# Attention outputs in 64x64 tiles: one block of queries on its own 64 rows, masks on the diagonal squares only

## The chip, the cores and the metric

One Trainium2 chip, one of its NeuronCores. The metric is the device time of one execution of the whole program, in microseconds (us). A run gives the median of several executions; beside it one execution is recorded by the hardware profiler.

Engines are named as in the profile: PE is TensorE (matmuls), PEld its weight loads, DVE is VectorE, ACT is ScalarE, POOL is GpSimd, SP issues most of the transfers.

## The reference

Two layers over 1024 tokens of width 1024: a retention/RWKV layer, then an attention layer, each followed by a SwiGLU network. The change lies in the attention layer alone:

```python
def swa_sink_mixer(h, w_qkv, b_qkv, sinks, w_o, b_o):
    ...
    z = h @ w_qkv + b_qkv
    q, k, v = jnp.split(z, [SWA_WIDTH, SWA_WIDTH + SWA_KV_HEADS * HEAD_DIM], axis=-1)
    ...
    kb, vb = with_prev(k), with_prev(v)
    s = jnp.einsum('bnqhgd,bnkhd->bnhgqk', q, kb).astype(jnp.float32) * HEAD_DIM ** -0.5
    qi = jnp.arange(W)[:, None]
    kj = jnp.arange(2 * W)[None, :]
    rel = qi + W - kj
    band = (rel >= 0) & (rel < W)
    ...
    m = jnp.maximum(jnp.max(s, axis=-1, keepdims=True), sink)
    e = jnp.exp(s - m)
    p = e / (jnp.sum(e, axis=-1, keepdims=True) + jnp.exp(sink - m))
    o = jnp.einsum('bnhgqk,bnkhd->bnqhgd', p.astype(vb.dtype), vb)
    return o.reshape(B, T, SWA_WIDTH) @ w_o + b_o
```

Sixteen heads of 64 in four groups share four key and value heads. Queries come in blocks of 128 (W); a query sees itself and the 127 tokens before it, so of the 256 keys of its own and the previous block exactly 128 are in its window. Cut into squares of 64 queries by 64 keys, a block has eight: two are empty, two are full, and four lie on a diagonal (two of the own block, two of the previous one).

## The kernel before, in words

The attention stage works on two halves of 512 tokens (`hf` 0 and 1). `proj` makes queries, keys and values: 24 matmuls of 512 columns for each of 12 tiles, their weights split into a high and a low part (ACT casts, L431; DVE subtracts, L432), the sum taken out of PSUM by DVE (L1635) and ACT (L1636). `kv` turns the values into token rows `vt` by PE transposes against `c_ident` (L1670), four for each of two value tiles, copied out by ACT (L1671).

The attention itself runs over 16 pairs: half, group of four heads, two blocks of queries. Each pair goes through four steps, which `ATTN_PLAN` writes into the program as S, D, M and O with the pair's number:

- S (`scores`): 24 score matmuls in 64x64 tiles (L1718; 20 where a half begins), into the PSUM banks r, c and two m. ACT copies the keys' part out (L1731), DVE puts the own block's keys over it by a mask (`copy_predicated`, L1732). So one row of 128 slots holds, slot by slot, either the own key or the previous block's. DVE takes the maximum (L1750) and the sink (L1751, L1752); ACT makes eight exponentials with their sums (L1755) and that of the sink (L1753); DVE adds and inverts (L1756, L1757); POOL and DVE multiply half each (L1759); DVE transposes in 32x32 pieces (L1765), and a transfer carries the tile to DRAM.
- D (`fetch`): four transfers bring it back as `pc`, key slots on the partitions.
- M (`sides`): DVE multiplies all 1024 columns by a mask (L1779: own keys); DVE and POOL subtract 512 each (L1784: previous keys). Both sides lie in `pT`.
- O (`out`): eight matmuls (six where a half's first block has no previous one), 128 key slots by 64 head columns by 256 query columns in full fp32, into the bank y (L1797); ACT casts them out (L1803), DVE takes the rest (L1804).

Small letters in `ATTN_PLAN` fill the time between: q, k, r are half-steps of the projections, w the output projection of half 0 (L446 to L449), f the norm that opens the second network (`form0`: `normed` L1247, then `split` L461 and L463), p half-steps of `ffn_early` (its first half is copied out by ACT at L1465 before the second half accumulates).

PE's order in the stage is written out: `K.queue(mark, ATTN_ORDER)` numbers the PSUM tiles in the order of their first use and chains the matmuls as the string says (`17:12` is twelve of tile 17, `18,19:12` twelve in turn from two tiles). The order on the other engines is the scheduler's. Bank f has three buffers, m two, r, c and y one each.

Of the kernel before, what the change touches and what calls it, by code (L numbers as in the profile page):

```python
# [16 lines left out]
P = 128  # L17
# [15 lines left out]
for _n, _w in (  # L33
# [9 lines left out]
    ("dmask", 1024), ("qdec", 512), ("kdec", 8), ("gam", 4), ("amask", 256), ("eps", 4),  # L43
# [9 lines left out]
def make_consts():  # L53
# [45 lines left out]
    put("amask", np.concatenate([np.where(x[:, None] == x[None, :], own, 0.0), own.T], axis=1))  # L99
# [155 lines left out]
class Kern:  # L255
    def __init__(self, ctx, tc, A, out):
# [20 lines left out]
        self.bd = self.dram("bd", [KT, P, HT])  # L277
        self.u0d = self.dram("u0", [NP, 2, P, HT])
# [972 lines left out]
    def form0(self, g, r, n8, sp):  # L1251

        self.X = {nm: [self.hl(n8, k + o) for k in range(4)] for nm, o in (("11", 0), ("21", 4))}
        for k in range(4):
            for nm, kk in (("11", k), ("21", k + 4)):
                f = self.t(sp, [P, HT], "u0", 4)
                self.normed(f, 0, kk, g, r)
                self.nc.sync.dma_start(self.bd[kk], f)
                self.split(f, *self.X[nm][k], False)

# [112 lines left out]
    def ffn_early(self, L, p, sp, banks):  # L1373

        u = self.uses(L, p, sp)
        g = []
        for i, nm in enumerate(("gate", "up")):
            w = self.wload(self.A[f"w_{nm}{L}"][2 * p])
            u0 = self.t(sp, [P, HT], "u0", 4)
# [42 lines left out]
    def ffn_pair(self, L, p, sp, next_w, form, x):  # L1422

        u = self.uses(L, p, sp, x)
        self.nc.sync.dma_start(x["11"], self.hid[2 * L][2 * p])
        u0s, gens = [], []
        for i in range(2):
            u0s.append(self.t(sp, [P, HT], "u0", 4))
# [182 lines left out]
    def attn_open(self, ap):  # L1611
        nc = self.nc
        m = self.const(ap, "amask").rearrange("p (m o t) -> p m o t", m=2, o=1)
        self.own = m[:, 0].rearrange("p o (x t) -> p o x t", x=2).to_broadcast([P, 2, 2, 64]).bitcast(mybir.dt.uint32)
        self.key = m[:, 1].rearrange("p o (q t) -> p q o t", q=4).to_broadcast([P, 4, 8, 32])
# [8 lines left out]
        self.pk = self.pvt = None  # L1624
        self.akv, self.aq, self.ch = {}, ([], []), {}
# [12 lines left out]
    def kv(self, hf, nr, ap):  # L1638
# [4 lines left out]
        vt = self.t(ap, [P, 5, 256], "vt", 2)  # L1643
# [15 lines left out]
        if hf:  # L1659
            G.tensor_copy(vt[:, 0, :], pvt[:, 4, :])  # L1660
        vcs = []
        for i in range(2):
            vc = self.t(self.pp, [P, HT], "nq", 4)
            yield from self.proj(nr, 10 + i, vc, bias=self.col("bqkv", 10 + i))
            vcs.append(vc)
            yield
        for i, vc in enumerate(vcs):
# [16 lines left out]
    def attn(self, ap, outs, fill, plan):  # L1684
# [52 lines left out]
        def scores(j):  # L1737
# [15 lines left out]
            S.activation(es, es, AF.Exp)  # L1753
            for h in range(8):
                S.activation(s8[:, h], s8[:, h], AF.Exp, bias=m[:, h : h + 1], accum_out=den[:, h : h + 1])  # L1755
# [13 lines left out]
        def fetch(j):  # L1769
            pc = pcs[j] = self.t(ap, [P, 4, 8, 32], "pc", 1)  # L1770
            for k in range(4):
                nc.sync.dma_start(
                    pc[32 * k : 32 * k + 32].rearrange("p q h t -> p q (h t)"), ds[j][:, :, k].rearrange("q t x -> t q x")
                )

        def sides(j):
            pc = pcs[j]
            pT = pTs[j] = self.t(ap, [P, 2, 4, 8, 32], "pT", 1)
            x = V.tensor_tensor(out=pT[:, 1], in0=pc, in1=self.key, op=ALU.mult)  # L1779
            if j + 2 in sinks:  # L1780
                self.behind(x, sinks[j + 2])
            for i, e in enumerate((V, G)):
                h = slice(4 * i, 4 * i + 4)
                e.tensor_tensor(out=pT[:, 0, :, h], in0=pc[:, :, h], in1=pT[:, 1, :, h], op=ALU.subtract)  # L1784

        def out(j):
# [16 lines left out]
            S.copy(hi, po)  # L1803
            V.tensor_tensor(out=lo, in0=po, in1=hi.bitcast(F32), op=ALU.subtract)  # L1804
# [65 lines left out]
def trunk(tc, A, out):  # L1870
    with ExitStack() as ctx:
# [106 lines left out]
        def form():  # L1978
            K.form0("n2b", K.factor_of(0, sp, "f"), K.n8(K.pp), sp)
# [23 lines left out]
        close(ga)  # L2003
        gc, cb = K.pool("cb", "right")
# [9 lines left out]
        close(gs, gc)  # L2014
# [68 lines left out]
```

## Time and profile before

| | us |
|---|---|
| median of 3 runs | 2271.2 |
| lowest and highest | 2270.53, 2272.11 |
| the profiled execution, its own time | 2270.19 |
| its span in the trace | 2268.4 |

The busy shares of the page are PE 98%, DVE 74%, ACT 45% and POOL 45% of the span; the TensorE clock is granted at 0.996 on the mean. The attention stage lies between about 1332 and 1640 us of the span. An "idle" number in brackets behind an instruction is the time that its engine stood still just before it, with what ended the wait. Matmuls overlap, so the step from one start to the next tells what one costs, not its own duration.

### The profile page before, as it was taken

The page shows a single profiled execution, that of the slowest core. Times are in us where ns is not written, and L with a number is a line of the kernel's source. Part 1 is how long each engine was busy: PE and PEld are TensorE (multiplying, and loading weights), DVE is VectorE, ACT ScalarE, POOL GpSimd, SP SyncE. Part 2 cuts the span into 40 slices and gives each one's busy share as a digit, 9 for nine tenths or more (in the row PEclk, how much of TensorE's full clock was granted, in tenths as well). Part 3 has the DMA queues.
Part 4 walks back from the last instruction along what each step waited for, and adds up shares of the span by engine and source line. Part 5 has one row for each costly group of instructions (what it writes and reads, how often), then busy time and mean ns, then how long its engine had stood idle before and what let it go on. Part 6 is the DMA issues. An engine that isn't in the chain of part 4 may idle for free. (4 is left out here: it accounts for less than half of the span.)

```text
span 2268.4 us, 36181 instructions
## 1 busy us (share of the span) xinstructions
PE 2222.8 (98%) x13296; PEld 1785.8 (79%) x13296; DVE 1687.9 (74%) x2476; ACT 1012.2 (45%) x1914; POOL 1024.7 (45%) x800
## 2 busy tenths in 40 slices
PE   8999999999999999999999999899899999999998
PEld 6777777778878888888888887687688888888886
DVE  7877965876567358888886868977557788888866
ACT  5454544424455333333333466657344333333336
POOL 3123221202341057777777601214203677777676
PEclk9999999999999999999999999999999999999999
DMA  8565654444456555555667334435446455658663
GB/s 281 186 220 203 201 158 134 141 118 124 147 181 205 185 172 209 209 211 216 237 241 247 130 123 137 154 131 168 163 140 230 177 215 209 211 196 290 228 218 116
DMA packets 181856, 423.22 MB, mean 187 GB/s; under 512 B 44464, under 2 KB 55344, under 8 KB 181680
## 3 DMA queue, kind: packets, MB, share of 16 engines
q1 hardware_dynamic: 178272, 414.37, 53.1%
q10 hardware_dynamic: 2832, 4.45, 0.6%
q8 instruction: 105, 1.72, 0.3%
q0 software_dynamic: 576, 2.10, 0.2%
q14 instruction: 71, 0.58, 0.1%
HBM read 283.87 MB, written 131.60 MB: 183 GB/s over the span
## 5 line engine op out<-in xcount | busy, mean ns | idle before, releaser
L290 PE MATMUL ps_f<-n,w 128*128 128x512 f32 x1440 | 358.8, 403 | 8.8 <-ACT w L431 5.7
L290 PEld LDWEIGHTS ps_f<-n,w 128*128 128x128 f32 x1440 | 266.9, 189 | 83.5 <-issue 12.6
L432 POOL TENSOR_TENSOR w<-wr,w 128x512 fp32r<-128x512 f32 x63 | 86.7, 1383 | 294.3 <-ACT w L431 277.8
L431 ACT CAST w<-wr 128x512 fp32r<-128x512 f32 x231 | 140.8, 618 | 156.1 <-PE ps_f L449 50.1
L1299 PE MATMUL ps_f<-n,w 128*128 128x512 f32 x415 | 166.4, 401 | 7.7 <-ACT u L1465 7.7
L432 DVE TENSOR_TENSOR w<-wr,w 128x512 fp32r<-128x512 f32 x168 | 124.9, 746 | 62.3 <-ACT w L431 61.9
L1301 PE MATMUL ps_f<-n,w 128*128 128x512 f32 x415 | 163.9, 395 | 1.3 <-DVE n L463 1.3
L1302 PE MATMUL ps_f<-n,w 128*128 128x512 f32 x415 | 163.9, 395 | 0.0
L432 POOL TENSOR_TENSOR w<-wq,w 128x512 fp32r<-128x512 f32 x91 | 130.3, 1443 | 31.8 <-ACT w L431 31.8
L1299 PE MATMUL ps_m<-n,w 128*128 128x512 f32 x333 | 130.5, 392 | 0.0
L1301 PE MATMUL ps_m<-n,w 128*128 128x512 f32 x333 | 129.6, 389 | 0.0
L1302 PE MATMUL ps_m<-n,w 128*128 128x512 f32 x333 | 129.5, 390 | 0.0
L1309 DVE TENSOR_TENSOR nq<-ps_m,u 128x512 f32<-128x512 f32 x88 | 58.8, 684 | 92.5 <-PE ps_m L1302 92.4
L463 POOL TENSOR_TENSOR n<-nq,n 128x512 fp32r<-128x512 f32 x60 | 100.0, 1680 | 7.6 <-ACT n L461 7.6
L1494 POOL TENSOR_TENSOR w<-wd,w 128x512 fp32r<-128x512 f32 (+1 forms) x62 | 86.9, 1411 | 34.0 <-ACT w L1493 30.3
L1299 PEld LDWEIGHTS ps_f<-n,w 128*128 128x128 f32 x415 | 78.9, 190 | 29.6 <-ACT u L1465 9.0
L1301 PEld LDWEIGHTS ps_f<-n,w 128*128 128x128 f32 x415 | 78.9, 190 | 19.0 <-DVE n L463 2.2
L1302 PEld LDWEIGHTS ps_f<-n,w 128*128 128x128 f32 x415 | 78.9, 190 | 17.3 <-issue 0.7
L1299 PE MATMUL ps_m<-cb,w 128*128 128x512 f32 x236 | 91.9, 389 | 0.3 <-DVE nq L1309 0.3
L1301 PE MATMUL ps_m<-cb,w 128*128 128x512 f32 x236 | 91.8, 389 | 0.0
L1302 PE MATMUL ps_m<-cb,w 128*128 128x512 f32 x236 | 91.8, 389 | 0.0
L1494 POOL TENSOR_TENSOR w<-ws,w 128x512 fp32r<-128x512 f32 (+1 forms) x48 | 71.7, 1498 | 43.6 <-ACT w L1493 41.8
(535 smaller groups left out, 6348.8 us busy)
## 6 DMA issues: line engine op xcount, KB each, us to landing
hc<-n SPq DMA_DIRECT2D x84, 512.0 KB, 3.4
wsp<-w SPq DMA_DIRECT2D x54, 512.0 KB, 3.1
w<-wsp SPq DMA_DIRECT2D x54, 512.0 KB, 3.4
n<-hc SPq DMA_DIRECT2D x54, 512.0 KB, 6.5
wq<-in_w_gate SPq DMA_DIRECT2D x44, 512.0 KB, 4.2
u<-u SPq DMA_DIRECT2D x88, 256.0 KB, 2.9
ha<-hc SPq DMA_DIRECT2D x34, 512.0 KB, 5.2
hid<-n SPq DMA_DIRECT2D x66, 256.0 KB, 2.0
```

What stands on the lines that cost most here:

```text
L290: i = self.nc.tensor.matmul(out, lhsT, rhs, **kw)
L431: nc.scalar.copy(hi[:, :n], raw[:, c])
L432: self.lo.tensor_tensor(out=lo[:, :n], in0=raw[:, c], in1=hi.bitcast(F32)[:, :n], op=ALU.subtract)
L463: e.tensor_tensor(out=lo, in0=src, in1=hi.bitcast(F32), op=ALU.subtract)
L1299: i = mm(ps, hi, xh, start=first and k == 0, stop=False, skip_group_check=True)
L1301: mm(ps, hi, xl, start=False, stop=False, skip_group_check=True)
L1302: mm(ps, lo, xh, start=False, stop=last and k == len(w) - 1, skip_group_check=True)
L1309: self.last_add = V.tensor_tensor(out=o, in0=x, in1=y, op=ALU.add)
L1494: nc.gpsimd.tensor_tensor(out=lo, in0=v, in1=hi.bitcast(F32), op=ALU.subtract)
```

## The change

Seven edits, all in the attention stage:

- `vt` holds four kinds of value rows for each pair of blocks: the first and the second 64 tokens of the own block and those of the previous one, with the first block of the pair on partitions 0 to 63 and the second on 64 to 127. `kv` makes them by matmuls of 64 tokens against `c_ident` (L1690): 16 for each value tile of half 0, 14 for each of half 1, instead of four transposes.
- `fetch` lands the squares in the same manner: partitions by block, `pc` with the slots' two halves side by side, pieces of 512 B where they were of 1 KB.
- `sides` masks only the 512 columns of the diagonal squares (L1809) and subtracts the result from `pc` in place (L1812), both on DVE. `pc` and `pT` have two buffers each.
- `out` runs 20 matmuls of 64x64 tiles (16 where a half begins; L1833), one block of queries into bank y and the other into a bank of f, and leaves the empty squares out. Each bank is taken out by itself (L1841, L1842).
- The normalisation is one DVE multiply of 1024 columns (L1786); POOL has no part in it. The first exponential of a pair is pinned behind the sink's.
- `form0` goes through its 11 tiles first and its 21 tiles after, and the `u0` tiles lie in a slot of the queries during the stage and in a pool of their own behind it.
- `ATTN_PLAN` and `ATTN_ORDER` are new: the values of half 1 are made among the steps w, the norm f stands ahead of S12, and S13 follows S12.

```diff
-S8 O5 M6 D7 krr S9 O6 M7 D8 k S10 O7 M8 D9 wwwwwwww S11 rr f rrrr S12 O8 M9 D10 p S13 O9 M10 D11 pp S14 O10 M11 D12 p
-S15 O11 M12 D13 pp O12 M13 D14 p O13 M14 D15 p O14 M15 p O15 p
+S8 O5 M6 D7 rr S9 O6 M7 D8 rrr S10 O7 M8 D9 rwkwkw S11 wwwww rr f S12 S13 O8 M9 D10 p
+O9 M10 D11 p S14 O10 M11 D12 pp S15 O11 M12 D13 pp O12 M13 D14 p O13 M14 D15 p O14 M15 p O15 p
...
+    def u0(self, sp):
+        if self.u0s is None:
+            return self.t(sp, [P, HT], "u0", 4)
+        self.nu0 += 1
+        return self.u0s(self.nu0 % 4)
...
-        vt = self.t(ap, [P, 5, 256], "vt", 2)
+        vt = self.t(ap, [P, 2, 4, 256], "vt", 2)
...
-            pt = self.pst("m", [P, 4, P])
-            for b in range(4):
-                nc.tensor.transpose(pt[:, b, :], vc[:, P * b : P * b + P], self.cst["ident"])
-            nc.scalar.copy(vt[:, 1:5, P * i : P * i + P], pt)
+            ds = slice(P * i, P * i + P)
+            for prev in range(2):
+                pt = self.pst("m", [P, 2, 2, P])
+                for b in range(4 - prev * hf):
+                    for r in range(2):
+                        x, c = b + prev, P * b + 64 * r
+                        o = 64 * (x % 2)
+                        nc.tensor.matmul(
+                            pt[o : o + 64, x // 2 % 2, r], vc[:, c : c + 64], self.cst["ident"], start=True, stop=True,
+                            skip_group_check=True,
+                        )
+                for rs, m in ((slice(64, P), slice(0, 2)), (slice(0, 64), slice(1, 2))) if prev * hf else (every,):
+                    nc.scalar.copy(vt[rs, m, 2 * prev : 2 * prev + 2, ds], pt[rs, m])
...
-            for e, hh in ((G, slice(0, 4)), (V, slice(4, 8))):
-                e.tensor_tensor(
-                    out=s8[:, hh], in0=s8[:, hh],
-                    in1=den[:, hh].rearrange("p (h o) -> p h o", o=1).to_broadcast([P, 4, P]), op=ALU.mult,
-                )
+            V.tensor_tensor(
+                out=s8, in0=s8, in1=den.rearrange("p (h o) -> p h o", o=1).to_broadcast([P, 8, P]), op=ALU.mult
+            )
...
-            pc = pcs[j] = self.t(ap, [P, 4, 8, 32], "pc", 1)
+            pc = pcs[j] = self.t(ap, [P, 2, 4, 4, 32], "pc", 2)
...
-            x = V.tensor_tensor(out=pT[:, 1], in0=pc, in1=self.key, op=ALU.mult)
+            d = pc.rearrange("p r (x q) h t -> p (r x) (q h t)", x=2)[:, 0:4:3]
+            o = pT.rearrange("p x q h t -> p x (q h t)")
+            x = V.tensor_tensor(out=o, in0=d, in1=self.key, op=ALU.mult)
...
-            for i, e in enumerate((V, G)):
-                h = slice(4 * i, 4 * i + 4)
-                e.tensor_tensor(out=pT[:, 0, :, h], in0=pc[:, :, h], in1=pT[:, 1, :, h], op=ALU.subtract)
+            V.tensor_tensor(out=d, in0=d, in1=o, op=ALU.subtract)
...
-            po = self.pst("y", [P, 2, 2, P])
-            pv = pTs[j].rearrange("p k q (b i e) t -> p k b e i q t", b=2, e=2)
-            for i in range(2):
-                kbs = (1,) if hf == 0 and b0 + i == 0 else (1, 0)
-                for kb in kbs:
+            po = [self.pst(x, [P, 2, P]) for x in "yf"]
+            c, o = (x[j].rearrange("p r q (i e) t -> p r e i q t", e=2) for x in (pcs, pTs))
+            lo, hi, every = slice(0, 2), slice(2, 4), slice(0, 4)
+            parts = [
+                (0, lambda e: c[:, 0, e, :, hi], hi), (0, lambda e: o[:, 0, e], lo), (1, lambda e: o[:, 1, e], hi),
+                (2, lambda e: c[:, 0, e, :, lo], lo), (3, lambda e: c[:, 1, e], every),
+            ]
+            for y, (kind, src, x) in enumerate(parts):
+                for i in range(2):
+                    first = hf == 0 and b0 + i == 0
+                    if first and kind > 1:
+                        continue
+                    rs = slice(64 * i, 64 * i + 64)
                     for e in range(2):
                         mm(
-                            po[64 * e : 64 * e + 64, i], vt[:, b0 + i + kb, 64 * g : 64 * g + 64], pv[:, kb, i, e],
-                            start=kb == 1, stop=kb == kbs[-1], skip_group_check=True,
+                            po[i][64 * e : 64 * e + 64, :, 32 * x.start : 32 * x.stop],
+                            vt[rs, b0 // 2, kind, 64 * g : 64 * g + 64], src(e)[rs],
+                            start=y == 0, stop=y > 3 or first and y > 0, skip_group_check=True,
                         )
```

Two places in the order of the instructions matter below. The first is PE at the values of half 1. In these rows `ps_m` is the bank that the value rows go through, `nq` a value tile, and `ps_y` a pair's outputs. Before, from the outputs of pair 5 on:

```order
L1797 MATMUL ps_y_13816<-pT_13700,vt_12393 64x256 x8
L1670 MATMUL ps_m_13836<-c_ident_154,nq_13318 128x128 x4
L1299 MATMUL ps_f_13851<-n_1943_12697,w_13845 128x512
L1301 MATMUL ps_f_13851<-n_1947_12701,w_13845 128x512
L1302 MATMUL ps_f_13851<-n_1943_12697,w_13845 128x512
```

Now, at the same value tile:

```order
L456 MATMUL ps_f_14223<-n_2021_13184,wx_14220 128x512
L1690 MATMUL ps_m_14249<-c_ident_154,nq_13365 64x128 x8
L1690 MATMUL ps_m_14259<-c_ident_154,nq_13365 64x128 x6
L453 MATMUL ps_f_14276<-n_2018_13181,wx_14270 128x512
L455 MATMUL ps_f_14276<-n_2022_13185,wx_14270 128x512
```

The step has moved from directly behind S8 and O5, into the output projection (L453 to L456) behind S10 and O7, and four instructions have become 14.

The second is DVE at the norm `form0` with the pairs 12 and 13. In the rows below `st_14726` belongs to S12 and `st_14783` to S13, `n_2220` is the last tile of the norm, and `pc_14840` the squares of pair 9. Now:

```order
L1777 TENSOR_TENSOR st_14726<-st_14726,nsink_12335 128x8
L470 TENSOR_TENSOR n_2220_14656<-q_2201_14618,n_2216_14652 128x512
L1842 TENSOR_TENSOR n_2239_14807<-ps_y_14811,n_2235_14803 128x2x128
L470 TENSOR_TENSOR n_2220_14656<-q_2201_14618,n_2216_14652 128x512
L1842 TENSOR_TENSOR n_2239_14807<-ps_f_14812,n_2235_14803 128x2x128
L1776 TENSOR_REDUCE st_14783<-s_14746 128x8
L1778 TENSOR_TENSOR st_14726<-st_14726,sink_12333 128x8
L1809 TENSOR_TENSOR pT_14915<-pc_14840,c_amask_12331 128x512
L1777 TENSOR_TENSOR st_14783<-st_14783,nsink_12335 128x8
L1784 TENSOR_TENSOR st_14726<-st_14726 128x8
L1812 TENSOR_TENSOR pc_14840<-pc_14840,pT_14915 128x2x256
```

The subtraction of pair 9 (L1812), which its outputs need, stands behind the whole norm and behind L1784, which takes S12's sums from ACT. Before, the masks of a pair stood in the softmax of a later one with no norm between, as here those of pair 6 in S8's:

```order
L1750 TENSOR_REDUCE st_13795<-s_13758 128x8
L1751 TENSOR_TENSOR st_13795<-st_13795,nsink_12335 128x8
L1804 TENSOR_TENSOR n_2022_13164<-ps_y_13816,n_2018_13160 128x2x2x128
L1752 TENSOR_TENSOR st_13795<-st_13795,sink_12333 128x8
L1779 TENSOR_TENSOR pT_13827<-pc_13704,c_amask_12331 128x1024
L1784 TENSOR_TENSOR pT_13827<-pc_13704,pT_13827 128x4x128
L1756 TENSOR_TENSOR st_13795<-st_13795 128x8
```

On PE, the outputs of pair 9 (20 of L1833) now stand between the first and the second 24 matmuls of the network's first step, behind S12, ten projection matmuls, S13 and the outputs of pair 8.

## Rows read from the trace of the kernel before

**Rows 1.** The page's first part: busy us, share of the span, instructions.
```profile
PE 2222.8 (98%) x13296; PEld 1785.8 (79%) x13296; DVE 1687.9 (74%) x2476; ACT 1012.2 (45%) x1914; POOL 1024.7 (45%) x800
```

**Rows 2.** Windows: length; busy PE, PEld, DVE, ACT, POOL; PEclk; DMA, GB/s.
```profile
1388.00:1470.00 82.00, 73.98 (x584) 56.42 (x583) 77.76 (x126) 50.37 (x181) 21.42 (x16) 0.96 0.49 160
...
1541.00:1637.00 96.00, 85.78 (x578) 62.98 (x577) 60.96 (x87) 51.85 (x140) 37.71 (x28) 0.96 0.52 171
```

**Rows 3.** Waits of PE, 1340 to 1650 us: total us, times, longest us.
```profile
PE ps_f L1299 <- ACT u L1465: 8.1, 4, 6.5
PE ps_m L1670 <- DVE s L1732: 6.1, 2, 5.5
```

**Rows 4.** Timeline of PE, 1448 to 1476 us: start, us, instruction, [idle before].
```profile
1452.56 0.37 PE L1718 MATMUL ps_c<-ks,q 64*64 64x192 f32 x1
...
1454.06 0.65 PE L1797 MATMUL ps_y<-pT,vt 128*64 128x256 f32 x4
...
1462.39 1.12 PE L1670 MATMUL ps_m<-c_ident,nq 128*128 128x128 f32 x4 [5.48 <-DVE s L1732]
...
1463.74 0.63 PE L1301 MATMUL ps_f<-n,w 128*128 128x512 f32 x1
...
1471.96 1.52 PE L1797 MATMUL ps_y<-pT,vt 128*64 128x256 f32 x12
1474.06 0.66 PE L1670 MATMUL ps_m<-c_ident,nq 128*128 128x128 f32 x4 [0.58 <-DVE s L1732]
```

**Rows 5.** Timeline of DVE, one softmax section, 1436 to 1449 us.
```profile
1436.65 0.44 DVE L1732 COPY_PREDICATED s<-c_amask,ps_c 128x256 f32<-128x256 uint32 x1
1436.99 0.43 DVE L1732 COPY_PREDICATED s<-c_amask,ps_r 128x256 f32<-128x256 uint32 x1
...
1438.13 1.22 DVE L1750 TENSOR_REDUCE st<-s 128x8 f32<-128x1024 f32 x1
1439.39 0.17 DVE L1751 TENSOR_TENSOR st<-st,nsink 128x8 f32<-128x8 f32 x1
...
1442.97 0.28 DVE L1756 TENSOR_TENSOR st<-st 128x8 f32<-128x8 f32 x1 [0.88 <-ACT s L1755]
...
1444.13 1.53 DVE L432 TENSOR_TENSOR w<-wr,w 128x512 fp32r<-128x512 f32 x1
...
1446.18 1.23 DVE L1765 STREAM_TRANSPOSE sq<-s 128x1024 f32<-128x1024 f32 x1
1447.34 1.25 DVE L432 TENSOR_TENSOR wx<-wr,wx 128x512 fp32r<-128x512 f32 x2
1448.51 0.44 DVE L1732 COPY_PREDICATED s<-c_amask,ps_c 128x256 f32<-128x256 uint32 x1
```

**Rows 6.** Timeline, 1342 to 1349 us: PE on both sides of four transposes.
```profile
1344.04 0.39 PE L1299 MATMUL ps_f<-n,w 128*128 128x512 f32 x1
...
1344.62 0.48 PE L1301 MATMUL ps_f<-n,w 128*128 128x512 f32 x1
```

**Rows 7.** Timeline of PE, 1600 to 1608 us: a pair's eight output matmuls, what follows.
```profile
1603.13 1.95 PE L1797 MATMUL ps_y<-pT,vt 128*64 128x256 f32 x16
1605.01 0.50 PE L1299 MATMUL ps_f<-n,w 128*128 128x512 f32 x1
1605.35 0.40 PE L1301 MATMUL ps_f<-n,w 128*128 128x512 f32 x1
1605.58 0.39 PE L1302 MATMUL ps_f<-n,w 128*128 128x512 f32 x1
```

**Rows 8.** Timeline of PE, 1522 to 1566 us: the matmul of ones (the norm's sum).
```profile
1529.40 1.02 PE L478 MATMUL ps_f<-nq,c_ones 128*128 128x512 f32 x2
```

**Rows 9.** Timeline of ACT, the same stretch: the norm's first table load.
```profile
1531.08 1.28 ACT L479 ACT_TABLE_LOAD   x1
```

**Rows 10.** Timeline of DVE, the same stretch: the norm's products and differences.
```profile
1535.04 3.79 DVE L1247 SCALAR_TENSOR_TENSOR u<-h,pv,rs 128x512 f32<-128x512 f32 x4 [4.74 <-ACT rs L480]
1538.74 1.88 DVE L463 TENSOR_TENSOR n<-u,n 128x512 fp32r<-128x512 f32 x3
```

More of the change, by code (lines that the diff above doesn't have):

```diff
@@ L42 @@
     ("ident", 128), ("id2", 64), ("ones", 128), ("blk", 128), ("gmask", 128), ("smask", 512), ("cos", 1024), ("sin", 1024),
[L43 removed]
+    ("dmask", 1024), ("qdec", 512), ("kdec", 8), ("gam", 4), ("amask", 384), ("eps", 4),
 )
@@ L98, in make_consts @@
     x = np.arange(P) // 64
-    put("amask", np.concatenate([np.where(x[:, None] == x[None, :], own, 0.0), own.T], axis=1))
+    put("amask", np.concatenate([np.where(x[:, None] == x[None, :], own, 0.0), np.repeat(np.tile(own[:64, :64].T, (2, 1)).reshape(P, 2, 1, 32), 4, axis=2).reshape(P, 256)], axis=1))
     put("eps", np.tile(np.array([[RMS_EPS, RET_EPS, RWKV_EPS, math.log(0.5)]], np.float32), (P, 1)))
@@ L277, in __init__ @@
         self.bd = self.dram("bd", [KT, P, HT])
+        self.u0s = None
         self.u0d = self.dram("u0", [NP, 2, P, HT])
@@ L1253, in form0 @@
         self.X = {nm: [self.hl(n8, k + o) for k in range(4)] for nm, o in (("11", 0), ("21", 4))}
[L1254 to L1258, printed above, removed]
-                self.split(f, *self.X[nm][k], False)
+        for nm, o in (("11", 0), ("21", 4)):
+            for k in range(4):
+                f = self.u0(sp)
+                self.normed(f, 0, k + o, g, r)
+                self.nc.sync.dma_start(self.bd[k + o], f)
+                self.split(f, *self.X[nm][k], False)
+    def u0(self, sp):
[3 more added lines that the diff above has]
+        return self.u0s(self.nu0 % 4)
     def form1(self, g, r, n8, cb, ft):
@@ L1378, in ffn_early @@
             w = self.wload(self.A[f"w_{nm}{L}"][2 * p])
-            u0 = self.t(sp, [P, HT], "u0", 4)
+            u0 = self.u0(sp)
             g.append((self.early(self.pst(banks[i], [P, HT]), (lambda w=w: w[:4], lambda w=w: w[4:]), u0, u[i]), u0))
@@ L1427, in ffn_pair @@
         for i in range(2):
-            u0s.append(self.t(sp, [P, HT], "u0", 4))
+            u0s.append(self.u0(sp))
             self.nc.sync.dma_start(u0s[i], self.u0d[p, i])
@@ L1612, in attn_open @@
         nc = self.nc
-        m = self.const(ap, "amask").rearrange("p (m o t) -> p m o t", m=2, o=1)
-        self.own = m[:, 0].rearrange("p o (x t) -> p o x t", x=2).to_broadcast([P, 2, 2, 64]).bitcast(mybir.dt.uint32)
-        self.key = m[:, 1].rearrange("p o (q t) -> p q o t", q=4).to_broadcast([P, 4, 8, 32])
+        m = self.const(ap, "amask").rearrange("p (o t) -> p o t", o=1)
+        self.own = m[:, :, :P].rearrange("p o (x t) -> p o x t", x=2).to_broadcast([P, 2, 2, 64]).bitcast(mybir.dt.uint32)
+        self.key = m[:, :, P:].to_broadcast([P, 2, 256])
         self.sink = self.t(ap, [P, 16], "sink")
@@ L1624, in attn_open @@
         self.pk = self.pvt = None
+        self.nu0 = 0
         self.akv, self.aq, self.ch = {}, ([], []), {}
@@ L1666, in kv @@
             yield
+        every = slice(0, P), slice(0, 2)
         for i, vc in enumerate(vcs):
-            pt = self.pst("m", [P, 4, P])
-            for b in range(4):
-                nc.tensor.transpose(pt[:, b, :], vc[:, P * b : P * b + P], self.cst["ident"])
-            nc.scalar.copy(vt[:, 1:5, P * i : P * i + P], pt)
+            ds = slice(P * i, P * i + P)
[11 more added lines that the diff above has]
+                    nc.scalar.copy(vt[rs, m, 2 * prev : 2 * prev + 2, ds], pt[rs, m])
+            if hf and i:
+                G.tensor_copy(vt[:64, 0, 2:4, :], pvt[:64, 0, 2:4, :])
             yield
@@ L1752, in scores @@
             sinks[j] = V.tensor_tensor(out=es2, in0=m2, in1=heads(self.sink), op=ALU.add)
-            S.activation(es, es, AF.Exp)
+            x = S.activation(es, es, AF.Exp)
             for h in range(8):
-                S.activation(s8[:, h], s8[:, h], AF.Exp, bias=m[:, h : h + 1], accum_out=den[:, h : h + 1])
+                y = S.activation(s8[:, h], s8[:, h], AF.Exp, bias=m[:, h : h + 1], accum_out=den[:, h : h + 1])
+                if h == 0:
+                    self.behind(y, x)
             V.tensor_tensor(out=den, in0=den, in1=es, op=ALU.add)
             V.reciprocal(out=den, in_=den)
-            for e, hh in ((G, slice(0, 4)), (V, slice(4, 8))):
-                e.tensor_tensor(
-                    out=s8[:, hh], in0=s8[:, hh],
-                    in1=den[:, hh].rearrange("p (h o) -> p h o", o=1).to_broadcast([P, 4, P]), op=ALU.mult,
-                )
+            V.tensor_tensor(
+                out=s8, in0=s8, in1=den.rearrange("p (h o) -> p h o", o=1).to_broadcast([P, 8, P]), op=ALU.mult
+            )
             sq = self.t(ap, [P, 4, 8, 32], "sq", 1)
@@ L1769, in fetch @@
         def fetch(j):
-            pc = pcs[j] = self.t(ap, [P, 4, 8, 32], "pc", 1)
+            pc = pcs[j] = self.t(ap, [P, 2, 4, 4, 32], "pc", 2)
             for k in range(4):
+                b, k2 = k // 2, k % 2
                 nc.sync.dma_start(
-                    pc[32 * k : 32 * k + 32].rearrange("p q h t -> p q (h t)"), ds[j][:, :, k].rearrange("q t x -> t q x")
+                    pc[32 * k : 32 * k + 32].rearrange("p r q h t -> p r q (h t)"),
+                    ds[j][:, :, k2::2, P * b : P * b + P].rearrange("q t r x -> t r q x"),
                 )
@@ L1802, in out @@
             hi, lo = (n8[hf][x][:, :, tk].rearrange("p i (b t) -> p b i t", b=2) for x in (g, 4 + g))
-            S.copy(hi, po)
-            V.tensor_tensor(out=lo, in0=po, in1=hi.bitcast(F32), op=ALU.subtract)
+            for i in range(2):
+                S.copy(hi[:, i], po[i])
+                V.tensor_tensor(out=lo[:, i], in0=po[i], in1=hi[:, i].bitcast(F32), op=ALU.subtract)
             self.ch[hf] = [self.hl(n8[hf], k) for k in range(KT)]
@@ L1978, in form @@
         def form():
+            u = K.t(ap, [P, 4, HT], "q8", 2)
+            K.u0s = lambda i: u[:, i, :]
             K.form0("n2b", K.factor_of(0, sp, "f"), K.n8(K.pp), sp)
@@ L2003, in trunk @@
         close(ga)
+        gu, su = K.pool("su", "left")
+        K.u0s = lambda i: K.t(su, [P, HT], "u0", 4)
         gc, cb = K.pool("cb", "right")
@@ L2013, in trunk @@
         x, ts, X, W = ffn_late(1, sp, K.pp, opened)
-        close(gs, gc)
+        close(gu, gs, gc)
         gz, fz = K.pool("fz", "left")
```

4 lines of the change are left out of this document (1 added, 3 removed), and 22 rows, old and new, of the table ATTN_ORDER.

## The prediction

> **What bounds the kernel now.** I read the page first: PE is busy 98% of the span and the next engine, DVE, 74% [rows 1], so what counts is where PE stands still or does work that can go. Then PE by windows: in the attention stage it is idle 8.0 us of the stretch from 1388 to 1470 (82.0 less 73.98) and 10.2 us from 1541 to 1637 (96.0 less 85.78) [rows 2]. In the first of these DVE is busy 77.8 of 82 us, so DVE sets the pace there; in the last neither engine is full, and PE waits on chains.
>
> The waits name the places [rows 3]. One hole of 5.48 us is the value transposes of half 1: they need bank m, which DVE has not emptied, because DVE is behind PE by most of a softmax section [rows 4]. The other large one, 6.5 us, is a second half-step of the network waiting for ACT to copy out the first half [rows 3]. Behind the 5.48 us hole the matmuls run at the lower of the two clock levels: the granted clock of both stretches is 0.96 on the mean [rows 2]. With the 0.58 us in front of the second transposes [rows 4] and some 2.0 us for the slow matmuls (0.96 of 82 us gives 3.3 us away, part of it while PE stands still), the stretch from 1388 to 1476 loses 8.0 + 0.58 + 2.0 = 10.6 us of PE time. PE, then, gains by less work and by fewer holes, and the change touches both.
>
> **Outputs on PE.** Eight matmuls in two column halves run as 8 records in series, 1.95 us; six run as 6, 1.52 us [rows 7, 4]. So a 256-column record costs (1.95 - 1.52) / 2 = 0.215 us, and a matmul in full fp32, two records, 0.43. A block of queries now has four matmuls of 128 columns and one of 256, in its own rows, and the head columns choose the column half: four tiles, each with 4 x 0.215 + 0.43 = 1.29 us, against 8 x 0.215 = 1.72 today. That four such tiles run at once is what the scores show: 24 matmuls from 1452.56 to 1454.06 [rows 4], 1.5 us for tiles of 768 columns, which alone would take 1.29 each. Twelve pairs save 0.43; in the four pairs that open a half of one group the longest tile stays at 6 x 0.215 = 1.29 and nothing is saved (the six matmuls of today take as long). **-5.2 us.** Bounds: -6.9 if all sixteen gain, 0 if the gain is lost in hand-overs.
>
> A six-matmul group takes 1.52 where its records take 1.29, so 0.23 is paid around it for filling and draining [rows 4]. Outputs now follow the scores in the same tile shape; I take a quarter of that, 0.06 us for each of 16 pairs: **-1.0 us**, between 0 and -3.7. The Trainium skill (TensorEngine Tiling (Array Packing), section Key Properties) says that a change of the tiling mode drains the engine; by it a pair saves one of its two drains, and this term would be half of 0.23 times 16, -1.8.
>
> **Values on PE.** Four transposes cost 0.35 us (the next matmul starts 0.58 us after the last one instead of 0.23) [rows 6, 7]; four such groups are 1.4. They become 60 matmuls of 128 columns: 0.215 each, 12.9 us in series, 6.45 if the two column halves always overlap. Two in a row go to the same half, so they overlap in part; I take 7.5, nearer to the overlap that the outputs show. **+6.1 us**, between +5.0 and +11.5. It is paid in full: PE has no hole at either place in the new order, and before 1388 it is the bound.
>
> **DVE in the paced stretch.** From one section's first copy to the next is 11.86 us [rows 5]. Gone are POOL's halves of the work: beside them a subtraction of 0.63 us took 1.53 [rows 5]. The mask and the subtraction shrink from 1024 and 512 columns to 512 each. But between L1751 and L1756 lie 3.58 us (1439.39 to 1442.97), set by ACT's eight exponentials; today DVE fills all but 0.88 of it with the mask and the subtraction, and now these take only 1.2 there, so DVE waits longer. Behind it the normalisation doubles (about 1.15 for 1024 columns, by the transpose's step of 1.16), and a pair's outputs are taken out in two pieces. I add up the new section from the same steps: four copies 1.5, the maximum 1.2, the 3.6, two small ones 0.5, normalisation 1.15, transposes 1.15, an output piece 0.3, and four or five of 0.6 for the projections: 11.8 to 12.4. So the pace does not change. The value step leaves its place, but the lag that it met remains: O6 and O7 then wait for DVE to empty the banks of O5 and O6, which stands behind those 3.6 us, 3 and 2 us by the same addition. I count what is lost here at 9.9 instead of 10.6: **-0.7 us**, between -9.6 (only 1.0 us lost) and +2.
>
> **The norm and the steps behind it.** From the start of the ones matmul at 1529.40 [rows 8] the factor reaches DVE 5.6 us later today, and 3.96 after the first table load [rows 9, 10], which ACT's other work held back; I take 4.0. In the new order DVE then does, before the subtraction that O9 needs: 8 products at 0.93 (3.79 over four) and 8 differences at 0.63 (1.88 over three) [rows 10], eight predicated copies at 0.34 and two maxima at 1.2 [rows 5], a projection and four pieces of outputs and masks (2.4 together), five small ones (0.8): 20.7 us, so O9 starts no earlier than 24.7. PE has until then ones 1.0, S12 and S13 3.0, ten and 24 matmuls at 0.23 (7.8), O8 1.5: 13.3. It is idle 11.4 us. Two later holes remain as today, where the second half-step waits for eight exponentials and a table load: 3.2 together. 14.6 against 10.2: **+4.4 us**, between +1 (DVE's steps a sixth shorter) and +7 (the clock falls after both holes).
>
> The transfers of D move the same bytes in pieces half as large; they have two buffers now and land two steps before M, so I cost them at nothing; without that cover a landing would add some 3 us to a pair. The larger constant costs nothing: it is loaded once, ahead of the stage.
>
> **Sum:** -5.2 - 1.0 + 6.1 - 0.7 + 4.4 = +3.6 on the profiled execution's 2270.2, which stands 1.0 below the median of 2271.2. I forecast **2275 us**, and call anything within 0.2% (4.5 us, about what a measurement of this kernel can tell from none) no change.
>
> **Rivals.**
> 1. *DVE stops pacing: faster.* If the waits on ACT are filled and a section falls under PE's own time for a pair (36 matmuls of 0.23, scores 1.5 and outputs 1.5: 11.3 us), the lag never builds up and 9.6 of the 10.6 us come back. For it: POOL's slowing of DVE is gone, 0.9 us a section. Against it: the 3.58 us. +3.6 - 8.9 = -5.3: **2266 us**. It decides for itself at the section's length.
> 2. *The value matmuls run in series and the clock falls twice: slower.* Two consecutive ones share a column half, and PE takes its instructions in order. +11.5 instead of +6.1, and 12 more matmuls at 0.43 after the second hole, 2.4: **2283 us**. It decides if an L1690 group of 16 takes over 3 us.
> 3. *PSUM empties too slowly.* The outputs now borrow one of f's three banks from the projections; if a projection or an output waits some 0.7 us more at ten places where that bank's copy stands behind the exponentials, **2282 us**. The Trainium skill (TensorEngine Tiling (Array Packing), section PSUM Bottleneck) warns that tiling speeds up TensorE but not the emptying of PSUM. Rows cannot show it, since today only y is used.
> 4. *The four tiles do not run at once.* With two at a time a pair takes 2.58 instead of 1.72 and those with an empty block 1.93 instead of 1.29: 12 x 0.86 + 4 x 0.64 = 12.9 in place of -5.2: **2293 us**. The scores speak against it.
>
> **Chances.** My forecast 0.48, its own range 2270 to 2280; rival 1 0.28, rival 2 0.12, rival 3 0.09, rival 4 0.03. Of the forecast's share 0.28 lies within 0.2%, 0.17 above, 0.03 below; of rival 1's 0.20 is below and 0.08 within; of rival 3's 0.02 is within; the rest is above. Faster 0.23, the same 0.38, slower 0.39. The range from 2263 to 2284 takes in the first three rivals and leaves out the outer ends of rivals 1 and 2 and all of rival 4.
>
> **What would show it.** Outputs: 1.3 to 1.5 us for 20 matmuls. Values: a group of 16 in 1.7 to 2.3 us. Pace: the copies of successive sections 11.8 to 12.4 us apart, and DVE waiting on ACT in each. Norm: a PE hole of 6 to 7 us before O9, one of 4 to 5 before S13. I am wrong on the main point if PE is idle under 4 us between 1388 and 1476, or under 8 behind the ones matmul.

## The result, and the profile after

The changed kernel takes **2278.3 us** (median of 5 runs, 2277.2 to 2283.0) where the kernel before takes 2271.2: ratio 1.0037, 95% interval 1.0025 to 1.0048. It is slower by 7.1 us. The forecast was 2275 with a range of 2263 to 2284; the forecast itself, +3.8, was called no change, and +7.1 is one. The profiled execution took 2281.14, its span is 2279.4; profiled executions of this kernel lie 2 to 3 us above its median, while the one of before lies 1.0 below. So I compare single stretches and look at the medians for the verdict.

The page's first part, to be laid beside [rows 1]:

```profile
PE 2230.2 (98%) x13768; PEld 1796.5 (79%) x13768; DVE 1671.1 (73%) x2492; ACT 1016.4 (45%) x1936; POOL 982.5 (43%) x768
```

PE is as full as before; 42 us of POOL and 17 of DVE went, and no time came of it. Windows over the stage, columns as in [rows 2]:

```profile
1388.00:1470.00 82.00, 76.37 (x767) 60.92 (x767) 66.85 (x126) 49.59 (x181) 1.05 (x2) 0.98 0.52 165
1470.00:1541.00 71.00, 67.71 (x501) 54.88 (x500) 50.11 (x90) 38.87 (x122) 2.29 (x2) 0.95 0.38 124
1541.00:1637.00 96.00, 84.19 (x735) 64.67 (x734) 56.49 (x97) 57.56 (x153) 26.76 (x19) 0.95 0.52 170
```

In the paced stretch DVE is busy 66.9 of 82 us where it was 77.8, and PE still stands still for 5.6 and runs at the lower clock level for part of the next 71 us. DVE has become emptier without becoming faster: it waits. The five largest waits of PE in the stage, 1335 to 1665 us (total, times, longest):

```profile
PE ps_f L1312 <- ACT q L1478: 8.0, 4, 5.0
PE ps_f L1833 <- DVE n L1842: 3.4, 3, 1.9
PE ps_y L1833 <- DVE n L1842: 3.3, 1, 3.3
PE ps_c L1744 <- DVE s L1758: 2.5, 1, 2.5
PE ps_f L1312 <- DVE q L1649: 1.5, 1, 1.5
```

The hole at the values of half 1 [rows 3, 4] is gone. In its place stand waits for banks f and y, which DVE empties late (L1842 an output, L1649 a projection). The waits for ACT's early copies (L1478, before L1465) are 8.0 us in the sum where they were 8.1.

**Where the time went.** Three landmarks on PE cut the stage: the first value matmul, then the matmuls of ones of three norms. Between them the steps of the PE timeline give:

| stretch | before | after | difference | made up of |
|---|---|---|---|---|
| first value matmul to first ones | 17.88 | 22.55 | +4.67 | values of half 0 |
| first to second ones | 167.25 | 180.41 | +13.16 | 38 projection matmuls moved in, +8.7; values of half 1 +3.2; four outputs -1.7; eight hand-overs from scores to outputs -1.2; lost +4.2 |
| second to third ones | 154.89 | 146.42 | -8.47 | the 38 matmuls moved out, -8.7; eight outputs -3.4; three hand-overs -0.5; lost +4.1 |

Together +9.4. The values and the outputs, in rows of the PE timeline:

```profile
1344.80 2.07 PE L1690 MATMUL ps_m<-c_ident,nq 128*64 128x128 f32 x32
...
1348.72 1.14 PE L1690 MATMUL ps_m<-c_ident,nq 128*64 128x128 f32 x16 [0.72 <-ACT vt L1695]
1350.11 1.15 PE L1690 MATMUL ps_m<-c_ident,nq 128*64 128x128 f32 x16 [0.24 <-ACT vt L1695]
...
1500.07 2.02 PE L1690 MATMUL ps_m<-c_ident,nq 128*64 128x128 f32 x28
...
1614.13 0.33 PE L1833 MATMUL ps_y<-pc,vt 64*64 64x128 f32 x2
...
1615.60 0.50 PE L1312 MATMUL ps_f<-n,w 128*128 128x512 f32 x1
```

Sixteen value matmuls (32 records) take 2.0 us; the second tile of half 0 also waits twice for ACT to empty bank m. A pair's 20 output matmuls take 1.47 (1614.13 to 1615.60) where eight took 1.88 [rows 7].

### The profile page after: what moved, and what is told of

Same layout as the page of the kernel before. It is cut to its first block, busy times and chain, and to the rows that moved or that the text cites. A ratio compares the mean times of both kernels' runs of the same rounds, so it can differ in the third digit from the quotient of the medians.

```text
span 2279.4 us, 37055 instructions
## 1 busy us (share of the span) xinstructions
PE 2230.2 (98%) x13768; PEld 1796.5 (79%) x13768; DVE 1671.1 (73%) x2492; ACT 1016.4 (45%) x1936; POOL 982.5 (43%) x768
## 4 chain that ended last, share of the span: by engine, by line
PE 73%; DVE 11%; ACT 5%; DMA 4%; issue 3%; POOL 1%; SPq 1%; DVEq 0%; ACTq 0%; POOLq 0%
PE ps_f L297 8%; PE ps_m L1312 7%; PE ps_m L1314 7%; PE ps_m L1315 7%; PE ps_m L297 5%; PE ps_f L1312 5%; PE ps_f L1315 5%; PE ps_f L1314 5%; PE ps_f L453 2%; PE ps_f L455 2%; PE ps_f L456 2%; PE ps_r L1315 2%; PE ps_r L1312 2%; PE ps_c L1315 2%; PE ps_r L1314 2%
## 5 line engine op out<-in xcount | busy, mean ns | idle before, releaser
L1312 PE MATMUL ps_f<-n,w 128*128 128x512 f32 x419 | 168.1, 401 | 10.1 <-ACT q L1478 7.2
L439 DVE TENSOR_TENSOR w<-wr,w 128x512 fp32r<-128x512 f32 x168 | 119.2, 713 | 64.7 <-ACT w L438 64.4
L1314 PEld LDWEIGHTS ps_f<-n,w 128*128 128x128 f32 x419 | 79.5, 190 | 17.1 <-issue 1.1
```

Source lines behind the costliest of these rows:

```text
L439: self.lo.tensor_tensor(out=lo[:, :n], in0=raw[:, c], in1=hi.bitcast(F32)[:, :n], op=ALU.subtract)
L1312: i = mm(ps, hi, xh, start=first and k == 0, stop=False, skip_group_check=True)
L1314: mm(ps, hi, xl, start=False, stop=False, skip_group_check=True)
```

## Experiments

Each line in bold gives the median less that of the kernel before on the same chip, and in brackets what the same three stretches together give less before's 340.0 in the profiled execution. The changed kernel has +7.1 [+9.4].

### The same kernel again

> The changed kernel once more, unchanged, beside the kernel before. The ledger read from its first profile, from the values of half 0 to the sum of the next norm: values +7.8 us, outputs and their hand-overs -6.5, stretch paced by DVE +4.2 (lost 14.8 where 10.6 were lost), norm and what follows +3.6: +9.1 in an execution of 2281. Theory: the ledger repeats within 1 us a term, and the executions between 2277 and 2283 differ in how often the granted clock falls behind a hole. Rival: the first profile was an odd one, and the paced stretch loses 10 to 11 us as in the kernel before. Median 2276 to 2281 either way.

**+6.9 [+9.4].** The three stretches are 22.66, 180.34 and 146.36 us: the ledger repeats within 0.1, so the first profile was not an odd one. Between the first and second ones PE idles 7.6 us instead of 8.9 and loses 1.4 us more to long steps at the lower clock level: what is lost is one sum, however it falls on holes and slow matmuls. So it looks as if something other than PE fixes it; the next run tries one candidate for it.

### Casts ahead of the exponentials

```diff
-                S.copy(hi[:, i], po[i])
+                x = S.copy(hi[:, i], po[i])
+                if j < 8:
+                    for y in exps[j + 3]:
+                        self.behind(y, x)
```

> ACT's two casts of a pair's outputs pinned ahead of the exponentials of the pair three later (pairs 0 to 7); nothing else. Theory (the f bank of a pair's outputs is held until the next exponentials are done, and PE's next outputs and projections wait for it): PE's waits on the outputs' difference (L1842, 6.7 us in all) and the two clock falls behind them go, and 4 to 7 us come back: 2271 to 2274. Rival (DVE's section of 12.4 to 13.6 us against 11.3 of PE sets the pace, wherever it is felt): the waits move to the scores' banks c, r and m, the stretch loses as much, 2277 to 2280.

**+3.0 [+2.3].** 2275.1: 3.9 us less than the same kernel again, at the edge of what the theory gave; the stretch between the first two ones falls from 180.3 to 174.3. First what ACT does in the changed kernel, once the outputs of pair 1 have left PE at 1411.6:

```profile
1422.53 0.39 ACT L1781 ACTIVATE s<-s,st 128x128 f32<-128x128 f32 x1
...
1422.91 0.35 ACT L1841 CAST n<-ps_f 128x256 fp32r<-128x256 f32 x1
```

The cast of bank f stands behind the eighth exponential. DVE's difference follows it, and PE, which wants that buffer for pair 2, starts only then:

```profile
1423.36 0.37 DVE L1842 TENSOR_TENSOR n<-ps_f,n 128x256 fp32r<-128x256 f32 x1
```

```profile
1423.78 0.33 PE L1833 MATMUL ps_f<-pc,vt 64*64 64x128 f32 x2 [1.85 <-DVE n L1842]
```

The bank is held for 11.8 us. With the pin both casts of the next outputs stand in the time in which ACT waits for DVE anyway, ahead of the exponentials:

```profile
1422.01 0.39 ACT L1843 CAST n<-ps_y 128x256 fp32r<-128x256 f32 x1
1422.27 0.40 ACT L1843 CAST n<-ps_f 128x256 fp32r<-128x256 f32 x1
1424.35 0.21 ACT L1779 ACTIVATE st<-st 128x8 f32<-128x8 f32 x1 [1.68 <-DVE st L1778]
```

PE's waits for this difference in the stage fall from 6.7 to 3.5 us. They do not vanish, and the waits for a projection's bank (L1649) stay, 3.0 us where they were 2.8: part of the rival is right, DVE's section still sets a pace. Its length says how much:

| first copies of S3 and S9 on DVE | us | per section |
|---|---|---|
| before | 1400.39, 1472.91 | 12.09 |
| changed | 1404.95, 1480.42 | 12.58 |
| casts pinned | 1409.44, 1482.04 | 12.10 |
| values by transposes (below) | 1406.11, 1477.43 | 11.89 |
| normalisation split (below) | 1406.11, 1483.50 | 12.90 |
| one buffer (below) | 1405.65, 1485.74 | 13.35 |

The changed section is 0.49 us longer than that of before. Over these six sections that is 2.9 of the 4.2 us lost there; the pin takes it back: the differences of the outputs then lie in DVE's wait on the exponentials and not behind it, and DVE's waits for cast weights fall from 2.8 to 0.7 us in that stretch. What the pin gains beyond these 2.9 by the stretches (7.1 in all) was not taken apart further.

### The normalisation split again

```diff
-            V.tensor_tensor(
-                out=s8, in0=s8, in1=den.rearrange("p (h o) -> p h o", o=1).to_broadcast([P, 8, P]), op=ALU.mult
-            )
+            for e, hh in ((G, slice(0, 4)), (V, slice(4, 8))):
+                e.tensor_tensor(
...
```

> The changed kernel with the normalisation split again between POOL and DVE, 512 columns each, as before the change. Theory (in the paced stretch a DVE section has two waits, on the exponentials and for a cast weight, and it is the chain that is long, not DVE that is full): DVE's multiply falls from 1.22 to some 0.65 but the transpose behind it then waits for POOL's half of 1.25, so a section stays within 0.3 us and the median within 1.5 us of 2279. Rival (DVE's own work sets the section, and the change made it longer by the whole multiply): 0.6 us a section over nine sections, 4 to 5 us back, 2274.

**+10.3 [+10.2].** 2281.7, slower by some 3 us by the medians and 0.8 by the stretches. The intervals of the two ratios overlap (1.0029 to 1.0054, and 1.0021 to 1.0042 for the same kernel again), so the size of the loss is open; the 4 to 5 us that the rival wanted back are not there, and it falls. A section grows by 0.32 us, as near to the theory's 0.3 as can be told, but not by its mechanism: the transpose does not wait for POOL. DVE's own half takes 1.53 to 1.55 us in the six sections from 1425 to 1491 while POOL works on the other, where DVE alone takes 1.22 for both:

```profile
1451.15 1.55 DVE L1787 TENSOR_TENSOR s<-s,st 128x512 f32<-128x512 f32 x1
```

The 0.33 us between them are the growth of the section. Taking POOL out of this multiply is at least no loss.

### One buffer for the squares

```diff
-            pc = pcs[j] = self.t(ap, [P, 2, 4, 4, 32], "pc", 2)
+            pc = pcs[j] = self.t(ap, [P, 2, 4, 4, 32], "pc", 1)
...
-            pT = pTs[j] = self.t(ap, [P, 2, 2, 4, 32], "pT", 2)
+            pT = pTs[j] = self.t(ap, [P, 2, 2, 4, 32], "pT", 1)
```

> The changed kernel with one buffer each for the fetched squares and for the masked diagonal squares, as before the change, in place of two. Theory (a landing is then held back until the outputs that read the squares before are done, and DVE's masks, which stand in the middle of a section, wait for it in order): a section grows by up to 3 us where the landing is late, 2282 or more. Rival (the squares land two pairs ahead and one buffer is enough, as it was): within 1.5 us of 2279.

**+16.9 [+16.9].** 2289.7: the second buffers are worth 10 us by the medians, 7.5 by the stretches. It is mostly not the wait for a landing in the middle of a section that I expected (DVE has one, of 2.2 us, from 1385 to 1480); the masks leave their place in it. DVE in one section:

```profile
1447.46 0.17 DVE L1778 TENSOR_TENSOR st<-st,sink 128x8 f32<-128x8 f32 x1
1450.85 0.17 DVE L1784 TENSOR_TENSOR st<-st 128x8 f32<-128x8 f32 x1 [3.22 <-ACT s L1781]
...
1454.09 0.65 DVE L1809 TENSOR_TENSOR pT<-pc,c_amask 128x512 f32<-128x512 f32 x1
```

In the changed kernel, one section at about the same place:

```profile
1445.32 0.69 DVE L1809 TENSOR_TENSOR pT<-pc,c_amask 128x512 f32<-128x512 f32 x1
1446.04 0.69 DVE L1812 TENSOR_TENSOR pc<-pc,pT 128x512 f32<-128x512 f32 x1
1448.53 0.17 DVE L1784 TENSOR_TENSOR st<-st 128x8 f32<-128x8 f32 x1 [1.79 <-ACT s L1781]
...
1454.32 0.69 DVE L439 TENSOR_TENSOR wx<-wr,wx 128x512 fp32r<-128x512 f32 x1 [0.70 <-ACT wx L438]
```

Masks that lie between the sink and the sums are free here; behind the transpose they lengthen the section by 0.8. PE's outputs, too, now wait: 11.1 us in the sum for the masked squares (L1809 and L1812) and 4.5 in eight pieces for the landing itself. By the code the second buffer is needed because the outputs now read `pc` itself, which before was done with as soon as it was masked; `pc` and `pT` were not tried one by one.

### Values by transposes

The value tile is written with its tokens in another order, so that six of the eight groups of rows are 128 neighbouring columns:

```diff
+                for r in range(2):
+                    c = 256 * r + 64 * prev
+                    nc.tensor.transpose(pt[:, 1 if prev else 0, r], vc[:, c : c + P], self.cst["ident"])
+                    if not prev:
+                        nc.tensor.transpose(pt[:, 1, r], vc[:, c + P : c + 2 * P], self.cst["ident"])
...
```

> Value rows made by six transposes and four 64-column matmuls for a value tile of half 0 (six and two in half 1), where 16 and 14 matmuls stood; DVE writes the value tile with its tokens in another order for it. Theory (PE pays the value step in full): 2.0 us a tile become about 1.05, and 1.95 become 0.8; 4 us come back, 2274. Rival (the step is limited by the two m banks that ACT has to copy out): the waits on the copies grow by what the matmuls lose, under 1.5 us come back, 2277.

**+5.1 [+6.2].** 1.8 us less by the medians, which the intervals of the two ratios do not tell from none, and 3.1 by the stretches. PE in the first tile of half 0:

```profile
1346.71 0.27 PE L1692 MATMUL ps_m<-c_ident,nq 128*128 128x128 f32 x1
1346.82 0.27 PE L1694 MATMUL ps_m<-c_ident,nq 128*128 128x128 f32 x1
...
1347.04 0.27 PE L1694 MATMUL ps_m<-c_ident,nq 128*128 128x128 f32 x1
1347.14 0.27 PE L1692 MATMUL ps_m<-c_ident,nq 128*128 128x128 f32 x1
1347.35 0.44 PE L1698 MATMUL ps_m<-c_ident,nq 128*64 128x128 f32 x4
1347.72 0.33 PE L1692 MATMUL ps_m<-c_ident,nq 128*128 128x128 f32 x1
1347.97 0.44 PE L1698 MATMUL ps_m<-c_ident,nq 128*64 128x128 f32 x4
```

A transpose costs 0.11, but at the two changes to and from the 64-column matmuls that can be read here a step is 0.21 and 0.25: the change of the tile's shape adds 0.10 to 0.14. So a tile of half 0 takes 1.6 instead of the expected 1.05, and one of half 1 1.6 where 1.95 stood. Of the theory's 4 us the value step itself gives 1.4: 0.75 in the first stretch and twice 0.33 in the second. The wait for bank m is 1.07 where both were 0.96, so the rival's mechanism does not hold, although its 2277 is what was measured.

The rest of the stretches is another effect, which the edit did not aim at: the second stretch falls from 180.4 to 173.9 and the third grows from 146.4 to 150.6. The order on DVE and ACT is the scheduler's, and it changed with the edit. In the changed kernel the difference of bank f stands behind L1784, which takes the exponentials' sums; here it stands ahead of the same instruction (L1792), without any pin. The changed kernel, then this one:

```profile
1435.41 0.17 DVE L1784 TENSOR_TENSOR st<-st 128x8 f32<-128x8 f32 x1 [1.68 <-ACT s L1781]
...
1435.73 0.37 DVE L1842 TENSOR_TENSOR n<-ps_f,n 128x256 fp32r<-128x256 f32 x1
```

```profile
1433.28 0.42 DVE L1850 TENSOR_TENSOR n<-ps_f,n 128x256 fp32r<-128x256 f32 x1
...
1436.78 0.17 DVE L1792 TENSOR_TENSOR st<-st 128x8 f32<-128x8 f32 x1 [1.09 <-ACT s L1789]
```

A section is 11.89 us (table above), 0.69 shorter than in the changed kernel and more than the pinned casts give. So this run speaks for the account of the emptied banks as well, and it is no clean price of the values. Why 4.1 us are lost again behind the norm was not taken apart.

### S13 where it was

The plan and the order string with S13 behind the outputs of pair 8 and the first half-step, as before the change:

```diff
-... rr f S12 S13 O8 M9 D10 p
-O9 M10 D11 p S14 ...
+... rr f S12 O8 M9 D10 p
+S13 O9 M10 D11 p S14 ...
```

> S13 put back behind the outputs of pair 8 and the first half-step, where it stood before the change; the rest as in the changed kernel. Theory (the norm costs more because S13 comes while DVE is in the norm): the waits before S13 (2.5 and 0.7 us) and DVE's wait for the landing of pair 11's squares (2.2) go: 3 us come back, 2275. Rival (DVE's work of 20 us behind the norm is the bound, in whatever order): the outputs of pair 9 or the next half-step wait instead, within 1 us of 2278.

**+9.6 [+8.0].** 2281.7: 2.7 us more by the medians, with intervals that overlap, and 1.3 less by the stretches, so no gain. The waits before S13 go, and the longest one for an early copy grows from 5.0 to 7.5 us. The theory falls; the traces fit the rival, by which DVE and ACT behind the norm are late in either order, though the median is 2.7 above its 2278 to 2279 and not within 1.

### Exponentials behind the early copies

```diff
+        for j, c in ((14, 2), (14, 3), (15, 4), (15, 5)):
+            for y in exps[j]:
+                self.behind(y, self.cop[c])
```

`cop` holds ACT's copies of first half-steps (L1478) in the order of the program. In the changed kernel alone:

> The changed kernel with one addition: the exponentials of pairs 14 and 15 behind the copies of the half-steps of the network beside them (L1478), as in e6_all, without the other values and without the pinned casts. Theory (three separate losses that add): the holes of 5.0 and 1.1 us and the lower clock behind the first go, 5 to 7 us: 2272 to 2274. Rival (in e6_all these pins only gained because DVE's lag was smaller by then): the outputs and scores behind them wait instead, 2276 or more.

**+0.8 [+2.5].** 2273.7; against the kernel before beside it, 6.1 us better than the same kernel again: the theory. The last stretch falls from 146.4 to 140.0. PE's waits for the copies fall by 6.1 us there and its idle time by 3.8, so some 2.3 come back as waits for ACT's and DVE's next steps; the other 2.7 of the gain lie in the matmuls behind the hole, 48 records in 11.3 us where they took 13.5 without the wait, in part at a granted clock of 0.50 (1590.5 to 1594.0). The kernel before has the same defect at 1597.72 [rows 3], and the same pin there, for pair 15 alone:

> The kernel before, with the exponentials of pair 15 alone pinned behind the two copies of the half-step beside them. Theory: the hole of 6.47 us at 1597.72 is only ACT's order; it and some 2 us of lower clock behind it go, and the exponentials come 0.6 later: 2264 to 2266. Rival: the later softmax makes the outputs of pairs 14 and 15 wait by as much, 2271.

**-2.9 [-2.9].** 2268.5 (ratio 0.9986, 0.9978 to 0.9994): about half of what was expected. The hole becomes 2.4 us for ACT's next step, and the outputs of the last pairs wait 1.8 in pieces. Both accounts are partly right.

### Together

> The value rows of e2 and the pinned casts of e3 together, and the exponentials of pairs 14 and 15 pinned behind the copies of the half-steps of the network that stand beside them (L1478 in the changed kernel). Theory (three separate losses: the value matmuls 4 us, the held f bank 4 us, and PE's hole of 5.0 us at 1590.9 with 2 us of lower clock behind it, where a copy stands behind the exponentials): they add, 2279 less 2 less 4 less 5: 2268, 4 us under the kernel before. Rival (DVE's lag is what has to be paid, and what is won ahead comes back as waits of the outputs behind pair 12): no better than 2273.

**-4.4 [-4.4].** 2267.0 (ratio 0.9977, 0.9967 to 0.9986). By the medians the three gains of 1.8, 3.9 and 6.1 add to 11.8, and together they bring 11.3, from +6.9 to -4.4. By the stretches 3.1, 7.1 and 6.9 would be 17.1, and together they are 13.8. The copies behind the exponentials are a loss of their own; the other two are not separate, for both shorten the same section of DVE, by 0.69 and 0.48 us, and together by 0.97 (to 11.61). The longest hole left on PE is a wait of 2.8 us for the copy behind pair 13's exponentials:

> e6_all with the exponentials of pair 13 pinned too, behind the copies of the first half-step of the network: its hole of 2.8 us at 1563.9. Theory: 2 to 3 us come back, 2264.5. Rival (pair 13's softmax is what pairs 11 to 13 and DVE wait for next): nothing comes back, 2267 or more.

**-10.1 [-7.8].** 2262.7 (ratio 0.9956, 0.9943 to 0.9970): the theory, and more. This kernel beats both, and the kernel before with its own pin too. In its stage no wait of PE for ACT's early copies is left; the longest ones (L1754 is the scores' line there, L1845 the outputs', L1857 their difference):

```profile
PE ps_c L1754 <- DVE s L1768: 3.1, 2, 2.5
PE ps_y L1845 <- DVE n L1857: 2.8, 3, 1.8
```

## Why the prediction came out as it did

The measured time lies in the range, on the slower side of the forecast: four of the five terms have about the right size, one of them by luck, and one is wrong. By its terms, on the profiled executions:

- **Outputs, -5.2:** right; -5.1 (twelve pairs at 0.42, four at nothing). Rival 4 (four tiles don't run at once) is out.
- **Hand-overs, -1.0:** -1.7. From the start of scores to the outputs behind them it is 1.35 where it was 1.50, 0.15 at eleven places; I took 0.06 at sixteen. With the rule cited from the Trainium skill (TensorEngine Tiling (Array Packing), section Key Properties) I had -1.8, as 0.115 at sixteen places; the trace agrees with the rule in kind, and with the sum only because a larger price meets fewer places. The steps of 0.10 to 0.14 at each change of shape in the values by transposes speak for it too.
- **Values, +6.1:** +7.9. The overlap was right (2.0 for a group of 16, forecast 1.7 to 2.3), so rival 2 is out by its own sign, though its other half, a clock that falls twice, came about behind the norm (below); missing were the 0.96 us of waiting for ACT's copies of bank m and a fill at five groups.
- **Paced stretch, -0.7:** wrong in sign, +4.2, and this is the step that failed. I added up 11.8 to 12.4 us for a section from busy times and one wait; it was 12.58, with the longer waits on the exponentials that were forecast (1.2 to 1.8 where they were 0 to 0.9), and in four of the six sections one of 0.7 for a cast weight that I had not put in: 2.8 us, as much as the six sections are longer by (2.9). And I took the late emptying of output banks as the lag of before in another place. O6 waits as forecast, 3.3 us for 3, for bank y; O7 does not. New are four waits of PE from O2 on, 5.6 us together, two for an output's bank f, which ACT held behind the exponentials, and two for a projection's, which DVE emptied late (L1649). That is rival 3, which I gave 0.09, with fewer and longer waits than its ten of 0.7. The rule named with it (the Trainium skill, same page, section PSUM Bottleneck) agrees with the trace in so far as PE waits 6.7 us for L1842. But the cast and the difference of a bank take 0.35 and 0.37 us, and about half of these waits went by an order on ACT alone: it is not the speed of emptying that failed but its place in a queue.
- **Norm and behind, +4.4:** +4.1, the right size by luck: two errors cancel. I took the subtraction behind the norm for pair 9's, and the words ahead of those rows say so; `pc_14840` is pair 10's. Pair 9 had been masked at 1520.7. So no hole of 6 to 7 us stands before O9 (it waits 0.5), and before S13 it is 3.2 instead of 4 to 5. My hole of 11.4 us is 3.7 in these two places. Against that I left 3.2 us for the waits on the early copies, "as today", although [rows 3] have 8.1 for them; they are 8.0. So PE idles 11.8 us behind the ones where I had 14.6, only 1.6 more than the 10.2 of before, and the other 2.5 of the 4.1 are slow steps: S13 and O8, behind the hole before S13, take 5.3 us without their waits (1555.3 to 1561.3) where scores with outputs take 2.8 elsewhere (1577.4 to 1580.2), with a granted clock of 0.50 from 1558.4 to 1561.2. Ahead of the longest wait for a copy, DVE does this:

```profile
1580.64 0.69 DVE L1809 TENSOR_TENSOR pT<-pc,c_amask 128x512 f32<-128x512 f32 x1 [2.21 <-DMA pc<-pd]
...
1582.57 0.45 DVE L1758 COPY_PREDICATED s<-c_amask,ps_c 128x256 f32<-128x256 uint32 x1
```

  Here a landing may cost something after all: DVE waits 2.2 us for squares, and pair 14's copies stand behind it. Whether this wait has a part in the 5.0 us hole was not tried by itself.
- **Transfers at nothing, with the cover of two buffers:** right as to the cover. Taken away, it cost 10 us, though mostly not by a landing's 3 us a pair but by the place of the masks.
- **Rival 1 (DVE stops pacing)** is out: from S3 to S9 no section is under 11.7 us.

The terms sum to +9.4 in the stage. The two profiled executions differ by 10.95, so 1.6 lie outside the three stretches and were not looked into; the medians differ by 7.1, because one profiled execution stands 2.8 above its median and the other 1.0 below.

## What to carry to other kernels

A PSUM bank that is borrowed for a short result is held until the engine that empties it comes to it: look at what stands ahead of the emptying in that engine's queue, not at how long the copy takes. When work is taken off a pacing engine, add up its waits with the work: what filled a wait was free, and its removal gains nothing. And identify the tile of a row by its consumer before building a wait on it. When an edit leaves the order on an engine to a scheduler, compare that order before reading the edit's price from the time: the values by transposes gained most where they had changed nothing by intent.

## What the runs showed of the hardware that was not expected

- Value matmuls of 64 stationary columns, two and two in the same column half, overlap almost in full: 0.125 us each in a group of 16 (2.0 us), where the prediction's price for one in series is 0.215, so that 0.108 would be full overlap.
- A DVE multiply of 512 columns took 1.55 us in six sections in which POOL multiplied the other 512 beside it, longer than the 1.22 of DVE alone for all 1024. In other sections of the same run it took 0.69, and POOL's half 1.46 where it took 1.04 there.
- Changing between 128x128 transposes and 64-column matmuls added 0.10 and 0.14 us at the two places read, as much as the transpose (0.11) itself.
- Idle time and low clock stand in for each other where another engine sets the pace: in two executions of the same kernel PE idled 8.9 and 7.6 us in one stretch of 180.4 and 180.3, at a mean granted clock of 0.97 and 0.96.
